# Linear attention on quarters of the array: keys by values, scores and state products without zero padding

## Chip, core and metric

The kernel runs on one core of one Trainium2 chip. The metric is the time of one execution on the device, in microseconds (us). The engines are named as the profile names them: PE is the tensor engine (PEld its weight loads), DVE the vector engine, ACT the scalar engine, POOL the general engine (GpSimd), SP the engine that issues most DMAs.

## What is computed

Two layers of a transformer over 256 latent tokens and 256 context tokens, width 1024. Each layer has a mixer of two parallel head groups (gated linear attention and neighbourhood attention), an output projection, and a channel mixer: dense in layer 0, the two best of eight experts in layer 1. The change touches the linear attention alone. Cut to that:

```python
def gla_chunk(q, k, v, g, s0):        # chunks of C = 64 tokens, 4 heads, dk = 64, dv = 128
    b = jnp.cumsum(g.reshape(B, H, n, C, dk), axis=3)
    b_ref = b[:, :, :, C // 2:C // 2 + 1, :]
    a = jnp.einsum('bhncd,bhnsd->bhncs', q * jnp.exp(b - b_ref), k * jnp.exp(b_ref - b))   # scores
    a = jnp.where(lower, a, 0.0)
    o = jnp.einsum('bhncs,bhnsv->bhncv', a, v)                                             # values
    b_last = b[:, :, :, -1:, :]
    ds = jnp.einsum('bhnsd,bhnsv->bhndv', k * jnp.exp(b_last - b), v)                      # keys by values
    # s <- exp(b_last) * s + ds over the chunks, from the context's last state on
    o = o + jnp.einsum('bhncd,nbhdv->bhncv', q * jnp.exp(b), s_prev)                       # state products
```

It is done in both directions (backward with the order flipped), the two outputs are added, and each head is normalised by its root mean square.

## The kernel before

The tokens stand in four blocks of 128 (`tt` 0 and 1 latent, 2 and 3 context), so a block holds two chunks, and the 128 partitions of a tile split at 64 into two chunks or two heads (`hpi` counts pairs of heads). `gla_parts` (L671) builds the linear attention; its generator `core` (L772) runs eight items, four steps by two directions `d`, with the blocks in the order 2, 3, 0, 1 forward and 3, 2, 1, 0 backward. An item has output where its block is in `qtts`: all eight in layer 0, the last four in layer 1, twelve together. For each item:

- `s0` splits the log gates into `ghi` and `glo`, `s1` sums them by matmul with constant triangles (L794, L804), turns the keys (L796), and makes `et`, `E` and `ke` on ACT and the products `klz`, `qez`, `ke` on DVE and `qb` on POOL. The names that end in z are padded: the two halves of the partitions are written into different columns, and the rest stays zero from a clearing at the start (`zt`, L680, with `zget` handing the cleared tiles out in turn).
- `s2` (L835) makes the scores into one bank of PSUM (L840), copies them under the causal mask into the cleared tile `aT` (L843), and makes keys by values into another bank (L849).
- `s3` (L866) takes a pair of items, one of each direction: `values` (L863) adds `aT` times `v` to the block's output bank, then for each of the two chunks the state products are added (L876) and `advance` (L886) makes the next state in a padded tile (L893 for the first, L895 afterwards). When both directions of a block are done, `normalise` (L900) empties its output bank.

The core is woven with the projections of the neighbourhood attention: `weave(G["core"](gc), chain(Stream(jobs).gen(), fill_core), 1)` (L1125) takes one step of projection work (L210 to L212, twelve passes of 512 columns) for each step of the core, and then, when those are used up, modulation work (L356). Apart from a few parts that are ordered by hand, the order within each engine's queue is made by a planner with a priority list, before the run and from its own costs; `s1` is marked urgent. PSUM has eight banks here, handed out from one pool (`ps`). Behind the core come the neighbourhood attention, the output projection and the channel mixer. The f32 operands of these matmuls are whole f32; L210 to L212 and the gate sums use a shorter form of f32 in split parts.

Of the kernel before, what the change touches and what calls it, by code (L numbers as in the profile page):

```python
# [9 lines left out]
F32 = mybir.dt.float32  # L10
# [6 lines left out]
P = 128  # L17
# [18 lines left out]
def make_consts():  # L36

    i = np.arange(P)
    s, c = i[:, None], i[None, :]
    same = (s // 64) == (c // 64)  # L40
    groups = {}

    def put(group, name, a):
        g = groups.setdefault(group, ([], {}))
        at = sum(x.shape[1] for x in g[0])
        a = np.asarray(a, np.float32)
        g[1][name] = (at, a.shape[1])
        g[0].append(a)

    put("base", "ident", np.eye(P))  # L50
    sel = np.zeros((P, 2))
    sel[i % 32 == 0, 0] = 1.0
    sel[i % 32 == 1, 1] = 1.0
    put("base", "sel", sel)
    put("base", "one", np.ones((P, 1)))
    put("base", "eps", np.full((P, 1), EPS))

    rot = np.zeros((P, P))
    for d in range(P):
# [12 lines left out]
    put("mix", "cos", cos)  # L72
    put("mix", "sin", sin)
    for nm, le, ref in (("F", s <= c, 32), ("B", s >= c, 31)):
        r = (c // 64) * 64 + ref
        le_ref = (s <= r) if nm == "F" else (s >= r)
        put("gla", "T" + nm, np.concatenate([(same & le) * 1.0 - (same & le_ref) * 1.0, (same & le) * 1.0], 1) / 16.0)
        put("gla", "R" + nm, (same & ~le) / 16.0)
    put("moe", "tri", s < c)
    put("moe", "iota", np.repeat(i[None, :], P, 0))  # L80
    put("moe", "fold", (s % 32) == np.arange(NE)[None, :])
    put("moe", "want", np.repeat(np.array([RANKS]), P, 0))
    return {k: (np.ascontiguousarray(np.concatenate(g[0], 1)), g[1]) for k, g in groups.items()}
# [10 lines left out]
def kernel(ctx: ExitStack, tc: tile.TileContext, A: dict, out: bass.AP):  # L94
# [576 lines left out]
    def gla_parts(l, full, qtts, nq_tok, C, W, mx, gl, nv, o_sb):  # L671
# [3 lines left out]
        v4 = gl.tile([P, 4, 512], F32, name="v4")  # L675
        v = [v4[:, tt, :] for tt in range(4)]

        zero = {}

        def zt(nm, shape, n):  # L680
            tiles = [gl.tile(shape, F32, name=f"{nm}_{i}") for i in range(n)]
            for t in tiles:
                nc.gpsimd.memset(t, 0.0)
            zero[nm] = [tiles, 0]

        def zget(nm):
            z = zero[nm]
            z[1] += 1
            return z[0][(z[1] - 1) % len(z[0])]

        zt("klz", [P, 2, 256], 2)
        zt("qez", [P, 2, 2, P], 2)
        zt("aT0", [P, 4, P], 1)
        zt("aT1", [P, 4, P], 1)
        zt("S0", [P, 2, 2, P], 2)
        zt("S1", [P, 2, 2, P], 2)

        def gates_load(ge):
            wlr = ge.tile([P, KD, 32], F32, name="wlr")
# [72 lines left out]
        def core(gc):  # L772
# [14 lines left out]
            def s1(it):  # L787
# [17 lines left out]
                                         start=i == 0, stop=i == 1)  # L805
                et = gc.tile([P, 256], F32, tag="et", bufs=2, name="et")
                nc.scalar.activation(et, pe[:, 0:256], AF.Exp)
                it["klz"] = klz = zget("klz")
                for c in range(2):
                    r = slice(64 * c, 64 * c + 64)  # L810
                    nc.vector.tensor_tensor(out=klz[r, c, :], in0=pe[r, 256:512], in1=et[r, :], op=ALU.mult)
                if not it["out"]:
                    E = gc.tile([P, 2, 2], F32, tag="Es", bufs=3, name="Es")
                    nc.scalar.activation(E, pb[:, 0:4].rearrange("p (a t) -> p a t", a=2), AF.Exp)
# [8 lines left out]
                at = P + (63 if d == 0 else 0)  # L823
                nc.vector.tensor_copy(Es, E[:, :, at:at + 65:64])
                it["dec"] = lambda hpi, c: Es[:, hpi, c:c + 1]
                it["qez"] = qez = zget("qez")
                for c in range(2):
                    r = slice(64 * c, 64 * c + 64)
                    nc.vector.tensor_tensor(out=qez[r, :, c, :], in0=qT[r, :, tok], in1=E[r, :, 0:P], op=ALU.mult)
                it["ke"] = En  # L830
                nc.vector.tensor_tensor(out=En, in0=kT[:, :, tok], in1=En, op=ALU.mult)
                it["qb"] = qb = gc.tile([P, 2, P], F32, tag="qb", bufs=3, name="qb")
                nc.gpsimd.tensor_tensor(out=qb, in0=qT[:, :, tok], in1=E[:, :, P:2 * P], op=ALU.mult)

            def s2(it):  # L835
                d, tt = it["d"], it["tt"]
                if it["out"]:
                    pa = ps()
                    for hpi in range(2):
                        nc.tensor.matmul(pa[:, hpi * 256:(hpi + 1) * 256], it["ke"][:, hpi, :],  # L840
                                         it["qez"][:, hpi].rearrange("p a t -> p (a t)"), start=True, stop=True)
                    it["aT"] = aT = zget(f"aT{d}")
                    nc.vector.copy_predicated(aT, W("T" + "FB"[d], P, P).bitcast(I32).unsqueeze(1).to_broadcast([P, 4, P]),  # L843
                                              pa.rearrange("p (a t) -> p a t", a=4))
                pd = ps()
                it["pdv"] = pdv = pd.rearrange("p (a c t) -> p a c t", a=2, c=2)
                for c in range(2):
                    for h in range(4):
                        nc.tensor.matmul(pdv[64 * (h % 2):64 * (h % 2) + 64, h // 2, c, :],  # L849
                                         it["klz"][:, c, h * 64:(h + 1) * 64], v[tt][:, h * P:(h + 1) * P],  # L850
                                         start=True, stop=True)

            def values(it):
                d, tt = it["d"], it["tt"]
                if it["out"]:
                    first = tt not in obank
                    if first:
                        obank[tt] = ps()
                        seen[tt] = 0
                    seen[tt] += 1  # L860
                    ob = obank[tt]
                    for h in range(4):
                        nc.tensor.matmul(ob[:, h * P:(h + 1) * P], it["aT"][:, h, :], v[tt][:, h * P:(h + 1) * P],  # L863
                                         start=first and h == 0, stop=False, skip_group_check=True)

            def s3(pair):  # L866

# [2 lines left out]
                for i in range(2):  # L870
                    cs = [(it, i if it["d"] == 0 else 1 - i) for it in pair]
                    for hpi in range(2):
                        for it, c in cs:
                            S = state[it["d"]]
                            if it["out"] and S is not None:
                                nc.tensor.matmul(obank[it["tt"]][64 * c:64 * c + 64, hpi * 256:(hpi + 1) * 256],  # L876
                                                 it["qb"][:, hpi, 64 * c:64 * c + 64], S[:, hpi].rearrange("p a t -> p (a t)"),
                                                 start=False, stop=False, skip_group_check=True)
                    for it, c in cs:
                        if it["step"] < 3 or i == 0:  # L880
                            advance(it, c)
                for it in pair:
                    if it["out"] and seen[it["tt"]] == 2 and it["tt"] in obank:
                        normalise(it["tt"], obank.pop(it["tt"]))

            def advance(it, c):  # L886
                d = it["d"]
                S, Sn = state[d], zget(f"S{d}")
                for hpi in range(2):
                    for h in range(2):  # L890
                        r = slice(64 * h, 64 * h + 64)
                        if S is None:
                            nc.vector.tensor_copy(Sn[r, hpi, h, :], it["pdv"][r, hpi, c, :])  # L893
                        else:
                            nc.vector.scalar_tensor_tensor(  # L895
                                out=Sn[r, hpi, h, :], in0=S[r, hpi, h, :], scalar=it["dec"](hpi, c)[r],
                                in1=it["pdv"][r, hpi, c, :], op0=ALU.mult, op1=ALU.add)
                state[d] = Sn

            def normalise(tt, bank):  # L900
                ob = bank.rearrange("p (h t) -> p h t", h=4)
                o4 = o_sb[tt].rearrange("p (h t) -> p h t", h=4)
                nc.scalar.activation(o4, ob, AF.Square)
                ss = gc.tile([P, 4], F32, tag="g_ss", bufs=1, name="g_ss")
                nc.vector.tensor_reduce(out=ss, in_=o4, axis=AX.X, op=ALU.add)
# [1235 lines left out]
```

## Time and profile before

| | before |
|---|---|
| time, median of 3 runs | 1880.4 us (1879.72 to 1882.68) |
| the profiled execution | 1879.96 us |
| its span (first to last instruction) | 1878.1 us |
| mean granted clock of PE | 0.984 of full speed |
| busy: PE, PEld, DVE, ACT, POOL | 1797.8, 1297.5, 1189.9, 922.7, 84.2 us |
| moved by DMA | 491.90 MB, mean 262 GB/s |

Busy time is the time in which an engine has at least one instruction under way. Matmuls are pipelined, so their durations overlap, and starts tell more than durations. The span is the profiled execution's own time without what lies before the first and behind the last instruction.

### The profile page before, as it was taken

The numbers are of one execution on the slowest core, as the hardware profiler recorded it, in microseconds if no ns is written. First come the engines' busy times: TensorE is split into PE (matmuls) and PEld (weight loads), VectorE is DVE, ScalarE is ACT, GpSimd is POOL, SyncE is SP. The second block draws the span as 40 slices with busy tenths as digits, with TensorE's granted clock in tenths as the row PEclk, the third lists the DMA queues.
The fourth block names the chain that finished last, engine by engine and source line by source line (L and its number), as shares of the span: only waits on it lengthen the run. The fifth ranks groups of instructions, "written<-read, shape, count | busy, mean of one in ns | idle before, by whom it ended". The sixth has DMA issues, their size and how long they took to land. (4 is left out here: it accounts for less than half of the span.)

```text
span 1878.1 us, 25461 instructions
## 1 busy us (share of the span) xinstructions
PE 1797.8 (96%) x8773; PEld 1297.5 (69%) x8773; DVE 1189.9 (63%) x1750; ACT 922.7 (49%) x1329; POOL 84.2 (4%) x103
## 2 busy tenths in 40 slices
PE   5999899999999998999899999999999999999995
PEld 3688566877788887787577853588886358888731
DVE  4457686478642345368879951599996249999701
ACT  3443376522222336443757831577774247777501
POOL 2100200110000002001000000000000000000000
PEclk8999999999999999999899999999999999999998
DMA  9432546267763332424299999999999999999996
GB/s 327 137 105 52 183 163 221 79 197 255 227 190 92 121 109 66 141 79 130 58 341 340 325 347 404 409 409 404 409 378 350 407 406 408 404 409 385 340 408 262
DMA packets 203321, 491.90 MB, mean 262 GB/s; under 512 B 29744, under 2 KB 71248, under 8 KB 203184
## 3 DMA queue, kind: packets, MB, share of 16 engines
q1 hardware_dynamic: 201152, 483.12, 71.0%
q0 software_dynamic: 2032, 7.08, 1.1%
q8 instruction: 71, 1.16, 0.3%
q14 instruction: 66, 0.54, 0.1%
HBM read 485.94 MB, written 4.98 MB: 261 GB/s over the span
## 5 line engine op out<-in xcount | busy, mean ns | idle before, releaser
L170 DVE TENSOR_TENSOR wl<-raw,wr 128x1024 fp32r<-128x1024 f32 x446 | 536.1, 1225 | 132.9 <-ACT wr L169 128.7
L169 ACT ACTIVATE wr<-raw 128x1024 fp32r<-128x1024 f32 x446 | 465.8, 1059 | 295.3 <-PE ps L211 152.0
L210 PE MATMUL ps<-wr,HR 128*128 128x512 f32 x736 | 299.3, 407 | 2.5 <-ACT wr L169 2.5
L211 PE MATMUL ps<-wl,HR 128*128 128x512 f32 x736 | 294.4, 400 | 7.5 <-DVE wl L170 6.5
L212 PE MATMUL ps<-wr,HL 128*128 128x512 f32 x736 | 292.3, 397 | 0.0
L210 PE MATMUL ps<-HR,wr 128*128 128x512 f32 (+1 forms) x592 | 220.3, 373 | 9.6 <-ACT HR L1979 6.2
L211 PE MATMUL ps<-HL,wr 128*128 128x512 f32 (+1 forms) x592 | 218.5, 369 | 3.4 <-POOL HL L521 1.7
L212 PE MATMUL ps<-HR,wl 128*128 128x512 f32 (+1 forms) x592 | 217.4, 367 | 0.5 <-DVE wl L170 0.5
L211 PEld LDWEIGHTS ps<-wl,HR 128*128 128x128 f32 x736 | 139.5, 190 | 47.0 <-DVE wl L170 14.7
L210 PEld LDWEIGHTS ps<-wr,HR 128*128 128x128 f32 x736 | 139.5, 190 | 40.5 <-issue 4.7
L212 PEld LDWEIGHTS ps<-wr,HL 128*128 128x128 f32 x736 | 139.2, 189 | 32.5
L210 PEld LDWEIGHTS ps<-HR,wr 128*128 128x128 f32 x592 | 111.6, 189 | 41.8 <-issue 8.6
L211 PEld LDWEIGHTS ps<-HL,wr 128*128 128x128 f32 x592 | 112.3, 190 | 23.6 <-DVE HL L1984 3.4
L212 PEld LDWEIGHTS ps<-HR,wl 128*128 128x128 f32 x592 | 112.4, 190 | 19.2 <-DVE wl L170 1.0
L1600 PE MATMUL ps<-raw,xw 128*64 128x512 f32 (+1 forms) x596 | 117.2, 536 | 2.2 <-DMA raw<-in_moe_w_gate 1.1
L1615 DVE TENSOR_TENSOR hid<-hid,ps 128x512 f32<-128x512 f32 (+1 forms) x47 | 31.3, 665 | 132.9 <-PE ps L1600 132.9
L210 PE MATMUL ps<-wr,tr 128*128 128x512 f32 x280 | 111.9, 400 | 0.0
L211 PE MATMUL ps<-wl,tr 128*128 128x512 f32 x280 | 110.6, 395 | 0.0
L212 PE MATMUL ps<-wr,tl 128*128 128x512 f32 x280 | 110.4, 394 | 0.0
L1600 PEld LDWEIGHTS ps<-raw,xw 128*64 128x64 f32 x596 | 40.7, 137 | 66.4 <-issue 53.3
L405 DVE SCALAR_TENSOR_TENSOR sums<-raw,condS,sums 128x512 f32<-128x512 f32 x98 | 71.6, 761 | 19.6 <-DMA raw<-in_w_ada 18.8
L1600 PE MATMUL ps<-raw,tw 128*64 128x512 f32 x272 | 67.2, 605 | 3.9 <-DMA raw<-in_moe_w_down 2.8
(368 smaller groups left out, 2433.6 us busy)
## 6 DMA issues: line engine op xcount, KB each, us to landing
raw<-in_moe_w_down SPq DMA_DIRECT2D x180, 512.0 KB
raw<-in_moe_w_gate SPq DMA_DIRECT2D x169, 512.0 KB
raw<-in_moe_w_up SPq DMA_DIRECT2D x167, 512.0 KB
raw<-in_w_ada SPq DMA_DIRECT2D x80, 512.0 KB
raw<-in_w_in SPq DMA_DIRECT2D x48, 512.0 KB
HR1w<-in_moe_w_up SPq DMA_DIRECT2D x24, 512.0 KB
raw<-in_ffn_w_gate SPq DMA_DIRECT2D x22, 512.0 KB
raw<-in_ffn_w_up SPq DMA_DIRECT2D x22, 512.0 KB
```

Source lines behind the costliest of these rows:

```text
L169: nc.scalar.activation(wr, raw, AF.Copy)
L170: nc.vector.tensor_tensor(out=wl, in0=raw, in1=wr.bitcast(F32), op=ALU.subtract)
L210: nc.tensor.matmul(o, lr, rr, start=start, stop=False)
L211: nc.tensor.matmul(o, lr, rl, start=False, stop=False)
L212: nc.tensor.matmul(o, ll, rr, start=False, stop=stop)
L405: nc.vector.scalar_tensor_tensor(out=o, in0=i_, scalar=s_, in1=o, op0=ALU.mult, op1=ALU.add)
L1600: nc.tensor.matmul(o[a * HALF:(a + 1) * HALF, 0:n], x, raw[:, a * n:(a + 1) * n], start=start, stop=stop)
L1615: nc.vector.tensor_tensor(out=hid, in0=hid, in1=st.pop((fb, 1))[:, 0:w], op=ALU.mult)
```

## The change

Score, key-value and state products are cut so that each matmul contracts over 64 partitions and writes 64 partitions: it uses a quarter of the array (a half of its rows by a half of its columns). What contracts over the lower half of the partitions goes to one PSUM bank and what contracts over the upper half to another. The padded tiles `klz`, `qez` and the padded states go; `aT` stays padded. Per item with output the scores are 8 matmuls of 64 columns instead of 2 of 256, key-value products 8 of 128 columns as before but over 64 partitions instead of 128, and the state products of one chunk and pair of heads 2 of 128 columns instead of 1 of 256. The scores share their two banks with the key-value products; the output of blocks `tt` and `tt + 1` shares two banks, split by head parity. A mask of 64 columns for each direction joins the constants.

```diff
+        put("gla", "M" + nm, le[:64, :64][i % 64] / 16.0)
...
-        zt("klz", [P, 2, 256], 2)
-        zt("qez", [P, 2, 2, P], 2)
-        zt("aT0", [P, 4, P], 1)
-        zt("aT1", [P, 4, P], 1)
-        zt("S0", [P, 2, 2, P], 2)
-        zt("S1", [P, 2, 2, P], 2)
+        keep = {}
+        for d in range(2):
+            keep[d] = gl.tile([P, 2, 2, P], F32, name=f"aT{d}")
+            nc.gpsimd.memset(keep[d], 0.0)
...
-                it["klz"] = klz = zget("klz")
-                for c in range(2):
-                    r = slice(64 * c, 64 * c + 64)
-                    nc.vector.tensor_tensor(out=klz[r, c, :], in0=pe[r, 256:512], in1=et[r, :], op=ALU.mult)
+                it["kl"] = et
+                nc.vector.tensor_tensor(out=et, in0=pe[:, 256:512], in1=et, op=ALU.mult)
...
-                it["qez"] = qez = zget("qez")
-                for c in range(2):
-                    r = slice(64 * c, 64 * c + 64)
-                    nc.vector.tensor_tensor(out=qez[r, :, c, :], in0=qT[r, :, tok], in1=E[r, :, 0:P], op=ALU.mult)
+                it["qe"] = qe = gc.tile([P, 2, P], F32, tag="qe", bufs=2, name="qe")
+                nc.vector.tensor_tensor(out=qe, in0=qT[:, :, tok], in1=E[:, :, 0:P], op=ALU.mult)
...
+            half = [slice(0, 64), slice(64, P)]
+
             def s2(it):
+
                 d, tt = it["d"], it["tt"]
+                banks = [ps() for _ in range(2)]
+                it["pdv"] = pdv = [b_[:, 0:256].rearrange("p (a t) -> p a t", a=2) for b_ in banks]
                 if it["out"]:
-                    pa = ps()
+                    pa = [b_[:, 256:384].rearrange("p (a t) -> p a t", a=2) for b_ in banks]
                     for hpi in range(2):
-                        nc.tensor.matmul(pa[:, hpi * 256:(hpi + 1) * 256], it["ke"][:, hpi, :],
-                                         it["qez"][:, hpi].rearrange("p a t -> p (a t)"), start=True, stop=True)
...
-                pd = ps()
-                it["pdv"] = pdv = pd.rearrange("p (a c t) -> p a c t", a=2, c=2)
-                for c in range(2):
-                    for h in range(4):
-                        nc.tensor.matmul(pdv[64 * (h % 2):64 * (h % 2) + 64, h // 2, c, :],
-                                         it["klz"][:, c, h * 64:(h + 1) * 64], v[tt][:, h * P:(h + 1) * P],
-                                         start=True, stop=True)
+                        for c in range(2):
+                            for a in range(2):
+                                nc.tensor.matmul(pa[a][half[c], hpi, :], it["ke"][half[a], hpi, half[c]],
+                                                 it["qe"][half[a], hpi, half[c]], start=True, stop=True)
+                    it["aT"] = aT = keep[d]
+                    mask = W("M" + "FB"[d]).bitcast(I32).unsqueeze(1).to_broadcast([P, 2, 64])
+                    for c in range(2):
+                        for a in range(2):
+                            nc.vector.copy_predicated(aT[half[c], :, a, half[c]], mask[half[c]], pa[a][half[c]])
+                for h in range(4):
+                    for c in range(2):
+                        nc.tensor.matmul(pdv[c][half[h % 2], h // 2, :], it["kl"][half[c], h * 64:(h + 1) * 64],
+                                         v[tt][half[c], h * P:(h + 1) * P], start=True, stop=True)
+
+            def o_bank(tt, a):
+
+                return obank[tt // 2][a][:, tt % 2 * 256:(tt % 2 + 1) * 256].rearrange("p (h t) -> p h t", h=2)
...
-                                nc.tensor.matmul(obank[it["tt"]][64 * c:64 * c + 64, hpi * 256:(hpi + 1) * 256],
-                                                 it["qb"][:, hpi, 64 * c:64 * c + 64], S[:, hpi].rearrange("p a t -> p (a t)"),
-                                                 start=False, stop=False, skip_group_check=True)
+                                for a in range(2):
+                                    nc.tensor.matmul(o_bank(it["tt"], a)[half[c], hpi, :], it["qb"][half[a], hpi, half[c]],
+                                                     S[half[a], hpi, :], start=False, stop=False, skip_group_check=True)
...
             def advance(it, c):
                 d = it["d"]
-                S, Sn = state[d], zget(f"S{d}")
-                for hpi in range(2):
-                    for h in range(2):
-                        r = slice(64 * h, 64 * h + 64)
-                        if S is None:
-                            nc.vector.tensor_copy(Sn[r, hpi, h, :], it["pdv"][r, hpi, c, :])
-                        else:
-                            nc.vector.scalar_tensor_tensor(
-                                out=Sn[r, hpi, h, :], in0=S[r, hpi, h, :], scalar=it["dec"](hpi, c)[r],
-                                in1=it["pdv"][r, hpi, c, :], op0=ALU.mult, op1=ALU.add)
+                S, Sn = state[d], gc.tile([P, 2, P], F32, tag=f"S{d}", bufs=2, name=f"S{d}")
+                if S is None:
+                    nc.vector.tensor_copy(Sn, it["pdv"][c])
+                else:
+                    for hpi in range(2):
+                        nc.vector.scalar_tensor_tensor(out=Sn[:, hpi, :], in0=S[:, hpi, :], scalar=it["dec"](hpi, c),
+                                                       in1=it["pdv"][c][:, hpi, :], op0=ALU.mult, op1=ALU.add)
...
-                nc.scalar.activation(o4, ob, AF.Square)
+                for a in range(2):
+                    nc.scalar.activation(o4[:, a], o_bank(tt, a), AF.Square)
...
-                nc.vector.tensor_tensor(out=o4, in0=ob, in1=y.unsqueeze(2).to_broadcast([P, 4, P]), op=ALU.mult)
+                for a in range(2):
+                    nc.vector.tensor_tensor(out=o4[:, a], in0=o_bank(tt, a),
+                                            in1=y[:, a:4:2].unsqueeze(2).to_broadcast([P, 2, P]), op=ALU.mult)
```

## Rows read from the trace of the kernel before

**Rows 1.** The page: the span, and the busy time of the tensor engine with its share of the span and its instructions.

```profile
span 1878.1 us, 25461 instructions
PE 1797.8 (96%) x8773; PEld 1297.5 (69%) x8773; DVE 1189.9 (63%) x1750; ACT 922.7 (49%) x1329; POOL 84.2 (4%) x103
```

**Rows 2.** Busy time by stretch: the two cores of the linear attention, and a stretch of the experts. The columns are the stretch, its length, the busy time of PE, PEld, DVE, ACT and POOL with their instructions, the granted clock, the busy share of the DMA engines, GB/s.

```profile
115.70:209.00 93.30, 93.30 (x585) 74.22 (x586) 62.95 (x145) 30.83 (x60) 8.60 (x12) 1.00 0.25 67
814.00:880.00 66.00, 66.00 (x488) 54.31 (x490) 48.34 (x110) 24.15 (x47) 4.00 (x6) 1.00 0.31 96
...
1200.00:1300.00 100.00, 100.00 (x444) 80.81 (x443) 91.46 (x85) 79.04 (x83) 0.00 (x0) 1.00 1.03 407
```

**Rows 3.** The instructions by tile, whole span: scores, key-value products and state products. The columns are the count of records, the duration in ns (least/median/most), first and last start, shapes.

```profile
L840 PE MATMUL ps<-qez,ke x48: 377/379/483, 131.5 to 874.3; 128*128 128x256 f32 x48
...
L849 PE MATMUL ps<-v,klz x256: 272/273/324, 132.5 to 875.4; 128*64 128x128 f32 x128
...
L876 PE MATMUL ps<-S,qb x88: 379/379/431, 147.3 to 879.4; 128*64 128x256 f32 x88
```

**Rows 4.** The tensor engine's instructions in order of time, layer 0. The columns are start, time from first start to last end, line, names, shapes and count of what is merged.

```profile
140.61 1.03 PE L840 MATMUL ps<-qez,ke 128*128 128x256 f32 x4
141.56 1.09 PE L849 MATMUL ps<-v,klz 128*64 128x128 f32 x16
142.59 0.50 PE L210 MATMUL ps<-HR,wr 128*128 128x512 f32 x1
142.93 0.40 PE L211 MATMUL ps<-HL,wr 128*128 128x512 f32 x1
...
145.46 1.95 PE L863 MATMUL ps<-v,aT 128*128 128x128 f32 x16
147.34 1.08 PE L876 MATMUL ps<-S,qb 128*64 128x256 f32 x8
148.35 0.50 PE L210 MATMUL ps<-HR,wr 128*128 128x512 f32 x1
...
171.62 1.95 PE L876 MATMUL ps<-S,qb 128*64 128x256 f32 x16
173.50 0.50 PE L210 MATMUL ps<-HR,wr 128*128 128x512 f32 x1
```

**Rows 5.** The same in a narrow window, 141.5 to 141.6 us.

```profile
141.56 0.33 PE L849 MATMUL ps<-v,klz 128*64 128x128 f32 x2
```

**Rows 6.** The same in layer 1, where key-value products of an item without output begin.

```profile
830.52 0.39 PE L211 MATMUL ps<-HL,wr 128*128 128x512 f32 x1
830.75 0.39 PE L212 MATMUL ps<-HR,wl 128*128 128x512 f32 x1
831.07 1.09 PE L849 MATMUL ps<-v,klz 128*64 128x128 f32 x16
```

**Rows 7.** The same in layer 1: gate sums with two columns and weights of 128 columns.

```profile
808.08 0.36 PE L804 MATMUL ps<-sums,ghi 128*128 128x2 f32 x2
808.30 0.36 PE L804 MATMUL ps<-sums,glo 128*128 128x2 f32 x2
```

**Rows 8.** The instructions of L807 (`et`), and what ended the scalar engine's idle time before them: us in total and times.

```profile
L807 ACT ACTIVATE et<-ps x16: 367/385/391, 116.8 to 866.2; 128x256 f32<-128x256 f32 x16
...
  PE ps L796: 34.5, 10
```

**Rows 9.** The vector engine's instructions on the tiles of the change, whole span; columns as in rows 3.

```profile
L811 DVE TENSOR_TENSOR klz<-ps,et x32: 409/422/428, 117.2 to 867.8; 64x256 f32<-64x256 f32 x32
...
L829 DVE TENSOR_TENSOR qez<-qT,E x24: 407/420/424, 119.0 to 868.7; 64x256 f32<-64x256 f32 x24
...
L843 DVE COPY_PREDICATED aT<-sums,ps x12: 732/741/747, 133.8 to 876.0; 128x512 f32<-128x512 int32 x12
...
L895 DVE SCALAR_TENSOR_TENSOR S<-S,Es,ps x96: 325/347/357, 138.7 to 877.7; 64x128 f32<-64x128 f32 x96
...
L893 DVE COPY S<-ps x16: 267/288/295, 137.4 to 834.3; 64x128 f32<-64x128 f32 x16
```

**Rows 10.** The tensor engine's instructions in order of time at the end of layer 0's core.

```profile
200.04 1.02 PE L840 MATMUL ps<-qez,ke 128*128 128x256 f32 x4
...
202.02 1.06 PE L356 MATMUL ps<-raw,condS 128*32 128x512 f32 x8
203.02 1.13 PE L840 MATMUL ps<-qez,ke 128*128 128x256 f32 x4
...
205.10 2.05 PE L863 MATMUL ps<-v,aT 128*128 128x128 f32 x16
207.09 1.95 PE L876 MATMUL ps<-S,qb 128*64 128x256 f32 x16
208.96 1.06 PE L356 MATMUL ps<-raw,condS 128*32 128x512 f32 x8
```

**Rows 11.** The squares of `normalise`; columns as in rows 3.

```profile
L903 ACT ACTIVATE x<-ps x6: 592/595/598, 173.6 to 880.3; 128x512 f32<-128x512 f32 x6
```

**Rows 12.** POOL in order of time, at the start of layer 1's mixer: the last cleared tiles but one, and a split of an activation.

```profile
733.15 1.45 POOL L683 MEMSET S<- 128x512 f32 x3
734.58 3.50 POOL L521 TENSOR_TENSOR HL<-n_h,HR 128x512 fp32r<-128x512 f32 x2
```

**Rows 13.** SP's DMA issues in order of time: the first loads of expert weights.

```profile
937.12 7.24 SPq L163 DMA_DIRECT2D raw<-in_moe_w_gate  x8
```

More of the change, by code (lines that the diff above doesn't have):

```diff
@@ L676, in gla_parts @@
         v = [v4[:, tt, :] for tt in range(4)]
[L678 to L689, printed above, removed]
-        zt("klz", [P, 2, 256], 2)
-        zt("qez", [P, 2, 2, P], 2)
-        zt("aT0", [P, 4, P], 1)
-        zt("aT1", [P, 4, P], 1)
-        zt("S0", [P, 2, 2, P], 2)
-        zt("S1", [P, 2, 2, P], 2)
+        keep = {}
+        for d in range(2):
+            keep[d] = gl.tile([P, 2, 2, P], F32, name=f"aT{d}")
+            nc.gpsimd.memset(keep[d], 0.0)
         def gates_load(ge):
@@ L839, in s2 @@
                     for hpi in range(2):
-                        nc.tensor.matmul(pa[:, hpi * 256:(hpi + 1) * 256], it["ke"][:, hpi, :],
-                                         it["qez"][:, hpi].rearrange("p a t -> p (a t)"), start=True, stop=True)
-                    it["aT"] = aT = zget(f"aT{d}")
-                    nc.vector.copy_predicated(aT, W("T" + "FB"[d], P, P).bitcast(I32).unsqueeze(1).to_broadcast([P, 4, P]),
-                                              pa.rearrange("p (a t) -> p a t", a=4))
@@ L855, in values @@
                 if it["out"]:
-                    first = tt not in obank
+                    first = tt // 2 not in obank
                     if first:
[L858 to L864, printed above, removed]
+                        obank[tt // 2] = [ps() for _ in range(2)]
+                    seen[tt] = seen.get(tt, 0) + 1
+                    for a in (1, 0):
+                        for hpi in range(2):
+                            h = 2 * hpi + a
+                            nc.tensor.matmul(o_bank(tt, a)[:, hpi, :], it["aT"][:, hpi, a, :], v[tt][:, h * P:(h + 1) * P],
+                                             start=first and hpi == 0, stop=False, skip_group_check=True)
             def s3(pair):
@@ L882, in s3 @@
                 for it in pair:
-                    if it["out"] and seen[it["tt"]] == 2 and it["tt"] in obank:
-                        normalise(it["tt"], obank.pop(it["tt"]))
+                    if it["out"] and seen[it["tt"]] == 2:
+                        seen[it["tt"]] = 3
+                        normalise(it["tt"])
             def advance(it, c):
                 d = it["d"]
-                S, Sn = state[d], zget(f"S{d}")
-                for hpi in range(2):
-                    for h in range(2):
-                        r = slice(64 * h, 64 * h + 64)
-                        if S is None:
-                            nc.vector.tensor_copy(Sn[r, hpi, h, :], it["pdv"][r, hpi, c, :])
-                        else:
-                            nc.vector.scalar_tensor_tensor(
-                                out=Sn[r, hpi, h, :], in0=S[r, hpi, h, :], scalar=it["dec"](hpi, c)[r],
-                                in1=it["pdv"][r, hpi, c, :], op0=ALU.mult, op1=ALU.add)
+                S, Sn = state[d], gc.tile([P, 2, P], F32, tag=f"S{d}", bufs=2, name=f"S{d}")
@@ L898, in advance, with normalise @@
+                if S is None:
+                    nc.vector.tensor_copy(Sn, it["pdv"][c])
+                else:
+                    for hpi in range(2):
+                        nc.vector.scalar_tensor_tensor(out=Sn[:, hpi, :], in0=S[:, hpi, :], scalar=it["dec"](hpi, c),
+                                                       in1=it["pdv"][c][:, hpi, :], op0=ALU.mult, op1=ALU.add)
                 state[d] = Sn
-            def normalise(tt, bank):
-                ob = bank.rearrange("p (h t) -> p h t", h=4)
-                o4 = o_sb[tt].rearrange("p (h t) -> p h t", h=4)
-                nc.scalar.activation(o4, ob, AF.Square)
+            def normalise(tt):
+                o4 = o_sb[tt].rearrange("p (h a t) -> p a h t", a=2, t=P)
+                for a in range(2):
+                    nc.scalar.activation(o4[:, a], o_bank(tt, a), AF.Square)
@@ L904, in normalise @@
                 ss = gc.tile([P, 4], F32, tag="g_ss", bufs=1, name="g_ss")
-                nc.vector.tensor_reduce(out=ss, in_=o4, axis=AX.X, op=ALU.add)
+                nc.vector.tensor_reduce(out=ss, in_=o_sb[tt].rearrange("p (h t) -> p h t", h=4), axis=AX.X, op=ALU.add)
                 y = rstd_of(gc, ss, 4, 1.0 / P)
-                nc.vector.tensor_tensor(out=o4, in0=ob, in1=y.unsqueeze(2).to_broadcast([P, 4, P]), op=ALU.mult)
+                for a in range(2):
+                    nc.vector.tensor_tensor(out=o4[:, a], in0=o_bank(tt, a),
+                                            in1=y[:, a:4:2].unsqueeze(2).to_broadcast([P, 2, P]), op=ALU.mult)
```

## The prediction

> **What bounds the kernel now.** I read the page first, then the busy time by stretch, then the tensor engine's instructions in order of time inside the two stretches that the change touches, then the vector engine's and the queues around them.
>
> The page gives a span of 1878.1 us with the tensor engine busy 96% of it [rows 1]. The profiled execution took 1879.96 us, 1.86 us more than its span and 0.44 us under the median of 1880.4 us; I work the sum against 1879.96 us. About 0.2% (3.8 us) is what a measurement of this kernel can tell from no change.
>
> The stretches tell where a gain would count [rows 2]. The linear-attention core runs from 115.7 to 209 us (layer 0) and from 814 to 880 us (layer 1). In both the tensor engine is busy without a gap (93.30 of 93.30 us, 66.00 of 66.00 us) at the full granted clock, 2.4 GHz, while the vector engine has 62.95 and 48.34 us of work and the DMA share is 0.25 and 0.31. So the tensor engine sets their length, and a microsecond of its work that goes is a microsecond of the stretch. From about 1000 us on the expert weights bound the kernel (DMA share 1.03 from 1200 to 1300 us), but their first loads are issued at 937.12 us [rows 13], behind both cores: what the cores save moves the whole expert part forward, and its length stays.
>
> **The unit of the sum.** Each f32 matmul stands in the trace as two passes: the scores of L840 are 24 matmuls in the program and 48 records, the key-value products of L849 128 and 256, the state products of L876 44 and 88 [rows 3]. Counts below are passes.
>
> What does a pass cost where halves of the array run side by side? Sixteen L863 passes on the whole array (128 columns) take 145.46 to 147.34, 0.1175 each. Eight L876 passes (256 columns, 64 weights wide) take 1.01 (147.34 to 148.35), sixteen take 1.88 (171.62 to 173.50): 0.87 for eight more, so a round of two passes is 0.2175 and 0.14 is fixed. Sixteen L849 passes (128 columns) take 1.03 (141.56 to 142.59); less 0.14 that is eight rounds of 0.11 [rows 4]. That two passes of a round run together is seen in a narrow window: two L849 passes fill 0.33 us, one of them up to 0.324 [rows 3, 5]. With four column groups of 32 it goes four wide: eight L356 passes of 512 columns take 1.00 (202.02 to 203.02) [rows 10], where eight on their own would take 8 x 4 x 0.1175 = 3.8. No row shows two row halves working side by side; that is the first unknown.
>
> Going into and out of the narrow forms costs too. An L849 group begins 0.32 behind the last whole-array pass (830.75 to 831.07) instead of 0.23 (830.52 to 830.75) [rows 6], so 0.09 at entry; 0.14 is inside, as above; and the first L210 afterwards lasts 0.34 instead of 0.23 (142.59 to 142.93) [rows 4], 0.11. A visit costs 0.34.
>
> **Scores, key-value products and their order (twelve items with output, eight in layer 0 and four in layer 1).** Before: 140.61 to 142.59 is 1.98, with the exit 2.09. After: 16 score passes of 64 columns in four rounds, 16 key-value passes of 128 columns in four rounds of 0.11. A score round lies between 0.055 and 0.11: streaming is half of 0.11, and the weights set a floor, since two-column passes with 128 columns of weights still start 0.11 apart (808.08 to 808.30, two of them) [rows 7], half of which I take for 64. I take 0.06, nearer the streaming row. Both parts now share two banks, and the masked copies must read the scores before the key-value products write the same bank: today `et` reads columns 0 to 255 of its bank, yet what ends its wait ten times is L796, which writes columns 256 to 511 of it [rows 8]. So the tensor engine leaves the narrow form between them and comes back, two visits: 2 x 0.34 + 4 x 0.06 + 4 x 0.11 = 1.36. Saved: 0.73, times 12, 8.8 us (8.8 + 0.2 to 8.8 - 2.4 for the bounds of the score round).
>
> The Trainium skill (TensorEngine Tiling (Array Packing), Instruction Overhead) speaks against the scores: some 60 cycles of overhead for each matmul, so that a dimension already small should not be split. By it sixteen passes would take, as an estimate at 2.4 GHz, 16 x 25 ns = 0.40 instead of 0.24, and the sum would be 1.9 us smaller. The trace does not agree for passes on different parts: the second L849 pass starts within 0.01 us of the first [rows 3, 5].
>
> **The four items without output (layer 1).** Eight rounds become four: 4 x 0.44 = 1.8 us.
>
> **State products.** 88 passes are 44 rounds of 0.2175; 176 passes of half the columns, four to a round, are 44 rounds of 0.11. Saved 44 x 0.1075 = 4.7 us. Values (L863) keep form and count.
>
> Gross: 8.8 + 1.8 + 4.7 = 15.3 us.
>
> **What is added, and its cover.** One masked copy of 0.74 becomes four on 64 partitions; the nearest rows, 64 x 128 with PSUM, take 0.29 (L893) and 0.35 (L895) [rows 9]. I take 0.35: 1.4 and a hand-over of 0.1 before the key-value products may start. In eight of the twelve items projection matmuls hide this: twelve passes of 0.23 make one step of 2.8 us. The copies can also queue behind a split of a weight on the vector engine, and the order was planned without knowing when they end. Below: nothing. Above: 8 x 2.7 = 21.6 us if nothing covers and a 1.2 us split stands ahead each time. The trace has the tensor engine fully covered now, so I take 0.25 an item, 2.0 us.
>
> The last pair of each core has no projection left. Today 200.04 to 208.96 is 8.92 us, all tensor work [rows 10]. Counted plainly it would become 8.92 - 2 x 0.73 - 8 x 0.1075 = 6.6. The chain scores (0.4), hand-over (0.1), eight copies (2.8), second key-value visit (0.7), values (1.99), states (1.0) gives 7.0; with slack I charge 0.5 for each core, 1.0 us.
>
> At each core's end two squares of 0.595 [rows 11] become four of half width, whose fixed part is paid twice more, and two tokens' outputs now share banks that both engines read. I charge 0.5 per core, 1.0 us (0 to 2).
>
> The vector engine loses work: half of the 32 `klz` and 24 `qez` products at 0.42, 48 of the 96 state updates at 0.35, three quarters of 16 copies [rows 9], against 36 more masked copies. None of it is priced, because no group of the tensor engine waits in these stretches. The cleared tiles that go are POOL's; in layer 1 POOL takes up its split 0.0 us behind the last of them (733.15 + 1.45, 734.58) [rows 12], so at most a few tenths are gained there. The constants grow by 128 columns, one copy of under 0.1 us.
>
> Net: 15.3 - 2.0 - 1.0 - 1.0 = 11.3; 1879.96 - 11.3 = **1868.7 us**.
>
> **Rivals.** *Row halves take turns* (0.18). Then scores need eight rounds (0.48), key-value eight (0.88), states 88 rounds of 0.11. An item is 0.68 + 0.48 + 0.88 = 2.04 against 2.09: nothing is won, the charges of 4.0 stay, about 1883.5 us (1879 to 1887). For it: no row shows row halves together. Against: column groups, four of them with four streams, do run together [rows 10].
>
> *The copies hold up the tensor engine* (0.08), which ends slower. Scores, copies and key-value products stand back to back in its queue; each item waits 1.5 us and whatever is ahead on the vector engine. One visit falls away (0.34 x 8 = 2.7), so it decides from (13.3 + 2.7) / 8 = 2.0 us an item; at 2.7 the time is 1879.96 + 21.6 - 16.0 = 1885.6 us. For it: the bank rule [rows 8]. Against: L849 groups are already broken up by other work. The Trainium skill (TensorEngine Tiling (Array Packing), PSUM Bottleneck) warns of this: tiling speeds the array but not what empties PSUM. No run here shows it yet.
>
> *All is covered* (0.10): no charges, score rounds at the floor, and the lighter vector engine shortens hand-overs: 1879.96 - 15.5 = 1864.5, down to 1858.
>
> *Given back later* (0.06): loads issued off the last filler work (202.02 and 208.96, L356 [rows 10]) set the next stage, so that the core's tail does not count: 1872 to 1879 us.
>
> **Numbers.** The forecast case has 0.58, alone 1862 to 1875. With the others the range is 1858 to 1884: it leaves out the ends of the first two rivals and little below. Faster by over 0.2%: 0.58 + 0.10 + half of the last, 0.70. Same 0.16, slower 0.14, mostly the first two rivals.
>
> **What would show it.** In the trace after: score and key-value passes starting in groups of four, 16 key-value passes in about 0.58; state groups of 32 in about 1.0; each core stretch shorter, layer 0 by about 7 us and layer 1 by about 4; first expert load near 926 us. Passes in pairs, a wait of the tensor engine on the masked copies, or a longer stretch from 209 to 235 us would make it wrong.

## The result, and the profile after

The changed kernel takes 1869.49 us (median of 4, 1868.96 to 1872.48) against 1881.07 us (1879.72 to 1882.68) for the kernel before on the same chip: a ratio of 0.9941, interval 0.9928 to 0.9954. The forecast was 1868.7 us. The profiled execution is the longest of the four, 1872.48 us. Lines are those of the changed kernel: scores L829, masked copies L835, key-value products L838, values L855, state products L869.

The page, to be read beside [rows 1]:

```profile
span 1870.7 us, 25857 instructions
PE 1784.4 (95%) x9005; PEld 1287.4 (69%) x9005; DVE 1161.8 (62%) x1704; ACT 922.9 (49%) x1335; POOL 75.4 (4%) x87
```

The two attention stretches by busy time (columns as in [rows 2]), from the first gate-sum pass to the last state pass:

```profile
118.20:205.10 86.90, 86.03 (x738) 67.42 (x740) 49.06 (x125) 31.14 (x62) 7.02 (x10) 1.00 0.29 72
803.60:870.90 67.30, 67.30 (x606) 55.70 (x607) 37.26 (x85) 26.97 (x52) 3.34 (x4) 1.00 0.34 101
```

Before, the same stretches ran from 115.77 to 209.03 us and from 806.79 to 879.77: 93.26 and 72.98 us. They are now 86.81 and 67.27 us (118.25 to 205.06, 803.61 to 870.88), 6.4 and 5.7 us less. The vector engine's 62.95 us [rows 2] is down to 49.06. Two later traces of the changed kernel (experiments 1 and 6 below) show the same two lengths within 0.1 us.

An item of layer 0 in order of time on the tensor engine (start, time to the last end, line, names), beside [rows 4]:

```profile
186.61 0.39 PE L213 MATMUL ps<-HR,wl 128*128 128x512 f32 x1
186.93 0.46 PE L829 MATMUL ps<-qe,ke 64*64 64x64 f32 x16
187.32 0.51 PE L211 MATMUL ps<-HR,wr 128*128 128x512 f32 x1
187.66 0.40 PE L212 MATMUL ps<-HL,wr 128*128 128x512 f32 x1
...
188.36 0.39 PE L212 MATMUL ps<-HL,wr 128*128 128x512 f32 x1
188.68 0.67 PE L838 MATMUL ps<-v,et 64*64 64x128 f32 x16
189.28 0.50 PE L213 MATMUL ps<-HR,wl 128*128 128x512 f32 x1
...
193.81 1.10 PE L869 MATMUL ps<-S,qb 64*64 64x128 f32 x32
194.84 0.50 PE L211 MATMUL ps<-HR,wr 128*128 128x512 f32 x1
```

From a group's start to the next instruction: scores 0.39 us, key-value products 0.60 (1.03 before), state products 1.03 (1.88 before). Four passes now share a round. Projection passes stand between scores and products, so an item enters the narrow form twice. The waits of the tensor engine in layer 0's stretch (who waited for whom, us in total, times, the longest); layer 1's has none:

```profile
PE ps L838 <- DVE aT L835: 0.9, 2, 0.6
```

Outside these stretches the change moves two more things. GpSimd clears eight tiles fewer, so its two transfers of 1.5 MB that fill a bias table (L334; L333 before, issued at 6.4 us) go out at 2.92 us, among the first loads. POOL in order of time:

```profile
1.96 0.43 POOL L332 MEMSET far<- 128x384 f32 x1
2.44 0.52 POOL L940 MEMSET ql<- 64x512 f32 x1
2.92 2.03 POOL L334 DMA_DIRECT2D rel<-far  x2
```

The low-rank passes that end the first stretch start at 67.25 us instead of 64.78. And after the first expert load, at 926.61 us instead of 937.12 [rows 13], part of the lead of 10.5 us goes: the first expert matmul comes 168.4 us later, before 165.7. Twenty microseconds from that stretch, first before, then after (columns as in [rows 2]):

```profile
957.10:977.10 20.00, 15.85 (x88) 12.60 (x87) 15.24 (x39) 10.31 (x22) 1.37 (x2) 0.83 0.81 280
```

```profile
946.60:966.60 20.00, 16.17 (x83) 12.68 (x84) 14.31 (x42) 8.96 (x21) 1.37 (x2) 0.70 0.75 252
```

The mean granted clock is 0.70 instead of 0.83 of 2.4 GHz. As an estimate, (0.83 - 0.70) x 20 = 2.6 us at full clock are missing there; that these are the 2.7 us is not shown (see the part on the prediction).

### The profile page after: what moved, and what is told of

Read it like the earlier page. It is cut to its first block, busy times and chain, and to the rows that moved or that the text cites. A ratio compares the mean times of both kernels' runs of the same rounds, so it can differ in the third digit from the quotient of the medians.

```text
span 1870.7 us, 25857 instructions
## 1 busy us (share of the span) xinstructions
PE 1784.4 (95%) x9005; PEld 1287.4 (69%) x9005; DVE 1161.8 (62%) x1704; ACT 922.9 (49%) x1335; POOL 75.4 (4%) x87
## 5 line engine op out<-in xcount | busy, mean ns | idle before, releaser
L171 DVE TENSOR_TENSOR wl<-raw,wr 128x1024 fp32r<-128x1024 f32 x446 | 535.1, 1222 | 140.6 <-ACT wr L170 137.1
```

What stands on the lines that cost most here:

```text
L171: nc.vector.tensor_tensor(out=wl, in0=raw, in1=wr.bitcast(F32), op=ALU.subtract)
```

## The experiments

All times are medians, with ratios to the kernel before measured on the same chip. The changed kernel itself, the neighbour of experiments 1 to 3, took 1868.67 us (ratio 0.9936, 0.9923 to 0.9949); the neighbour of 6 and 7, 1868.41 us (0.9950, 0.9936 to 0.9964). "Stretch" is as above; in these two runs it is 86.9 us in layer 0 and 67.2 to 67.3 in layer 1.

**1. The row halves in turns.** The loop over row halves goes outermost:

```
-for hpi in range(2):
-    for c in range(2):
-        for a in range(2):          # scores, row half a
+for a in range(2):
+    for hpi in range(2):
+        for c in range(2):
...
-for h in range(4):
-    for c in range(2):              # products, row half c
+for c in range(2):
+    for h in range(4):
```

and the state products likewise.

> The changed kernel with the same quarter matmuls, but ordered so that one half of the rows has all its passes before the other half. Theory (rounds of four quarters are the gain): rounds double. 12 items x 4 score rounds x 0.058 = 2.8, 16 x 4 key-value rounds x 0.11 = 7.0, 44 state rounds x 0.11 = 4.8, together 14.6 us: 1884 us (1880 to 1887), 16 key-value passes taking about 1.03 instead of 0.60. Rival (the gain came from the lighter vector engine and the missing padding): within 2 us of the changed kernel.

1875.17 us (0.9972, 0.9962 to 0.9982), 6.5 us slower: neither figure. The stretches take 91.6 and 69.7 us. The tensor engine in order of time:

```profile
188.18 0.47 PE L829 MATMUL ps<-qe,ke 64*64 64x64 f32 x16
...
190.36 0.66 PE L838 MATMUL ps<-v,et 64*64 64x128 f32 x8
190.94 0.50 PE L211 MATMUL ps<-HR,wr 128*128 128x512 f32 x1
...
195.93 1.16 PE L869 MATMUL ps<-S,qb 64*64 64x128 f32 x32
197.02 0.50 PE L211 MATMUL ps<-HR,wr 128*128 128x512 f32 x1
```

The edit undid the concurrency only in part. Eight products of one row half take 0.58 us (190.36 to 190.94), nearly as long as sixteen in the changed kernel: that is the price of two to a round. But scores (0.40) and state products (1.09) hardly lost, although written in turns: passes of the other row half ran beside them. So the run shows what the products lose when their halves part. Whether the other passes overtook one another or the planner had already put them in another order than the written one is open: the records do not name the quarter of a pass.

**2. The vector engine's work put back.** The products with `et` and `qe` and the state updates by row halves again, as the padded kernel had them; the masked copies stay four to an item, so the vector engine now has 66.3 us of work in layer 0's stretch, 3.3 more than in the kernel before:

```
-nc.vector.tensor_tensor(out=qe, in0=qT[:, :, tok], in1=E[:, :, 0:P], op=ALU.mult)
+for r in half:
+    nc.vector.tensor_tensor(out=qe[r], in0=qT[r, :, tok], in1=E[r, :, 0:P], op=ALU.mult)
```

> The changed kernel's matmuls, with the vector engine's work of the kernel before put back: key and query products in two halves of the partitions, each state update in four pieces of 64 partitions instead of two of 128, first states likewise. That is some 25 us of vector work more. Theory (the tensor engine sets the stretch): 0 to 1.5 us over the changed kernel. Rival (the lighter vector engine gave the gain): 5 to 11 us over it.

1879.1 us (0.9991, 0.9980 to 1.0002): 10.4 us slower, the rival's time, and the gain is gone. The stretches take 89.5 and 74.2 us, together 9.6 more than in the changed kernel. The waits for the copies are 2.6 us in layer 0 and 4.0 in layer 1 (0.9 and none in the changed kernel). The tensor engine in layer 1 (here scores are L831, products L840, copies L837, state updates L889), and the vector engine over the same time:

```profile
856.02 0.46 PE L831 MATMUL ps<-qe,ke 64*64 64x64 f32 x16
...
857.46 0.28 PE L213 MATMUL ps<-HR,wl 128*128 128x256 f32 x1
861.38 1.33 PE L840 MATMUL ps<-v,et 64*64 64x128 f32 x16 [3.64 <-DVE aT L837]
862.65 0.58 PE L211 MATMUL ps<-HR,wr 128*128 128x256 f32 x1
```

```profile
855.24 1.23 DVE L171 TENSOR_TENSOR wl<-raw,wr 128x1024 fp32r<-128x1024 f32 x1 [2.77 <-ACT wr L170]
...
857.42 0.85 DVE L798 TENSOR_TENSOR et<-ps,et 64x256 f32<-64x256 f32 x2
858.20 0.41 DVE L815 TENSOR_TENSOR qe<-qT,E 64x256 f32<-64x256 f32 x1
858.62 0.43 DVE L817 TENSOR_TENSOR ke<-kT,ke 128x256 f32<-128x256 f32 x1
859.07 1.42 DVE L889 SCALAR_TENSOR_TENSOR S<-S,Es,ps 64x128 f32<-64x128 f32 x4
860.52 1.01 DVE L837 COPY_PREDICATED aT<-sums,ps 64x128 f32<-64x128 int32 x4
```

The scores are done by 856.5 us, but their four copies stand behind the split of a projection weight (L171) and the eight pieces shown after it, and begin at 860.52; the products, which write the copies' bank, wait 3.64 us. The split was itself late, since the vector engine stood idle for 2.77 us until its weight was there. So the queue ahead of the copies, and not the pieces alone, makes this wait; a split ahead of the copies is what the prediction's upper bound named. After the idle time of the tensor engine sixteen products take 1.27 us instead of 0.60. The granted clock of the next 6.7 us is 0.58, most of it at the lower level of 1.2 GHz (columns as in [rows 2]):

```profile
861.30:868.00 6.70, 6.62 (x47) 6.17 (x51) 4.32 (x11) 1.97 (x5) 0.00 (x0) 0.58 0.27 78
868.00:874.00 6.00, 5.68 (x104) 4.24 (x101) 5.74 (x17) 1.33 (x2) 0.74 (x1) 1.00 0.15 22
```

The lower clock costs some (1 - 0.58) x 6.7 = 2.8 us there, as an estimate from that row. With the 5.7 us of waits more than in the changed kernel this makes 8.5 of the 9.6 us. So the lighter vector engine is what keeps the hand-over of the shared bank hidden. The Trainium skill (TensorEngine Tiling (Array Packing), PSUM Bottleneck) says that tiling speeds the tensor engine but not what empties PSUM; this run agrees, at 3.64 us in one place.

**3. Products ahead of the scores.** In `s2` the key-value products are issued first; nothing they write is then read by a copy before them.

> The changed kernel with the key-value products put ahead of the scores in each item, so that they need not wait for the masked copies and one visit to the quarter form is enough for both. Theory (a visit costs 0.34 us and the waits on the copies 0.9 in all): 12 x 0.34 + 0.9 = 5.0 us less, 1864.5 us (1862 to 1867). Rival (the visits are hidden, or what the core saves here is given back behind it): 1868 to 1871 us.

1864.96 us (0.9921, 0.9909 to 0.9933), 3.7 us less: inside the expected range, though the interval overlaps the changed kernel's. A second time, as the neighbour of experiments 4 and 5: 1866.11 us (0.9927, 0.9912 to 0.9941). In it layer 0's stretch is 82.9 us, 4.0 less than in the changed kernel, and an item is one visit to the narrow form (products L826, scores L833), 0.83 us to the next instruction instead of 0.39 + 0.60 and a second entry and exit:

```profile
182.28 0.67 PE L826 MATMUL ps<-v,et 64*64 64x128 f32 x16
182.77 0.41 PE L833 MATMUL ps<-qe,ke 64*64 64x64 f32 x16
183.11 0.50 PE L211 MATMUL ps<-HR,wr 128*128 128x512 f32 x1
```

Layer 1's stretch, where the theory had put four of its twelve visits, gains nothing (67.9 us): its last values wait 1.4 us for the copies, which are now issued later.

**4. Products first, and the vector work back.** The edits of 2 and 3 together.

> Keys-by-values passes ahead of the scores, and the vector engine's work put back as it was before the change: the query, key and state updates by row halves, some 13 us more of its work in layer 0 and 12 us in layer 1. Theory (the lighter vector engine matters only because the keys-by-values passes wait for the masked copies of the scores in their bank; with the order turned round nothing of the tensor engine waits for the copies except the values' tail): 0 to 3 us over the same order with the light vector work, 1865 to 1868, and the stall of about 3.6 us before the products in layer 1 is gone. Rival (the vector engine sets the length of the stretch by itself, through gates, decays and states): about 10 us over it, 1875, as it was when the same work was put back with the scores first, and the waits stand before other passes: scores, state passes or values.

1867.65 us (0.9938, 0.9926 to 0.9951), 1.5 us over its neighbour, the theory's time, and not to be told from it. In layer 0 the theory holds throughout, 83.9 us and no wait for the copies. In layer 1 it holds by half: the long stall before the products is gone, but its stretch is 5.0 us longer (72.9), with other waits, as the rival said:

```profile
PE ps L857 <- DVE aT L841: 4.0, 3, 1.7
PE ps L828 <- DVE S L889: 1.3, 1, 1.3
PE ps L782 <- DVE S L889: 0.7, 1, 0.7
```

Part of these 5 us is regained behind the stretch (2.6 us remain in the span).

**5 (two kernels). The transfers of the bias table.** Built on 3: the two score tiles are cleared five times over, which puts the transfers back to 6.7 us; and `clear_rel` is written after the low-rank step.

```
-        clear_rel(sp)
...
     G["low_rank"](ge)
+    if full:
+        clear_rel(ge)
```

> Keys-by-values passes ahead of the scores, and GpSimd sets the two score tiles to zero five times over instead of once: eight more sets of 128 x 512, as many as the kernel before spent on tiles that the change drops. They stand ahead of the two transfers of 1.5 MB that set the bias table in memory to its floor, so these go out near 6.4 us again and not at 2.9. Theory (the change let these two transfers go out ahead of the first loads of x and of the conditioning weights): the second group of x passes starts near 11.2 us again and not near 12.1, the low-rank passes of layer 0 start near 64.8 us and not near 66.3, and the time is 1 to 2 us less than the neighbour with one set, 1863 to 1864. Rival (the late start comes from something else, the loads of the first stretch sharing the rate of memory whatever the order): low-rank passes at 66 and the same time as the neighbour within 0.7 us.

> Keys-by-values passes ahead of the scores, and the two transfers that set the bias table to its floor are written after the low-rank step, behind the first stretch of loads. They move 3.15 MB, 12.7% of the sixteen engines' time in the first 60 us, at a time in which the transfers run at some 350 to 410 GB/s. Theory (the first stretch is bound by the loads): the low-rank passes of layer 0 start 4 to 8 us earlier, near 58 to 62 us, and the time falls by 3 to 8 us against the neighbour, to 1857 to 1862. Rival (the tensor engine and the scalar engine set the first stretch, or the transfers only move into the stretch of the bias table and the next loads): less than 1.5 us.

With the extra clears: 1867.66 us (0.9925, 0.9913 to 0.9938), not to be told from its neighbour, though the low-rank passes start at 63.75 us instead of 65.78 and the wait for the conditioning weights `w_ada` ahead of them falls from 6.6 us to 3.7. The first half of the theory holds; the 2 us do not reach the end (3.0 us ahead at the first expert matmul, 0.3 in the span; in one slice of the experts the granted clock is 0.95 against 0.97). Written behind the loads, the transfers are issued at 50.39 and 53.89 us, that wait is gone, and the low-rank passes start 8.8 us earlier:

```profile
50.39 1.13 POOL L334 DMA_DIRECT2D rel<-far  x1 [0.31 <-POOL far L332]
...
53.89 0.92 POOL L334 DMA_DIRECT2D rel<-far  x1
```

```profile
56.98 0.62 PE L701 MATMUL ps<-HR,wlr 128*32 128x512 f32 x1
```

1859.58 us (0.9886, 0.9872 to 0.9900), 6.5 us less. So the loads bind the first stretch: 3.15 MB fewer ahead of them, and the wait for them goes.

**6. Scores on the whole array again.** The rest as changed; padded queries, one masked copy for an item, a bank of their own.

> The changed kernel with its scores as they were before: four passes of 256 columns over the whole array into a bank of their own, queries padded by row half, one masked copy for an item instead of four; keys by values and state products stay on quarters. Theory (the scores on quarters are worth their passes: an item's scores took 0.95 us ahead of the products and now take 0.39 us and an entry of some 0.09; 12 items; against that the waits for the masked copies go, some 1.5 us): 2.5 to 5 us slower than the changed kernel, 1871 to 1873.5, of it some 3 us in layer 0. Rival (what the scores' passes gain is paid again by the bank that they share with the products and by the second entry, so that quarters for the scores are worth nothing): within 1 us of the changed kernel, or faster.

1867.0 us (0.9934, 0.9920 to 0.9947): not to be told from the changed kernel. Its stretches are 87.1 and 69.3 us, 0.1 and 2.0 longer; in layer 1 the tensor engine waits 1.4 us for a state update, which it does not in the changed kernel. By line in layer 0 (busy us, mean ns), first here, then the changed kernel:

```profile
L832 PE MATMUL ps<-qez,ke 128*128 128x256 f32 x32 | 8.3, 382 | 0.0
L840 PE MATMUL ps<-v,et 64*64 64x128 f32 x128 | 6.2, 283 | 0.0
```

```profile
L838 PE MATMUL ps<-v,et 64*64 64x128 f32 x128 | 5.9, 282 | 0.9 <-DVE aT L835 0.9
L829 PE MATMUL ps<-qe,ke 64*64 64x64 f32 x128 | 4.7, 231 | 0.0
```

The scores' passes are 3.6 us shorter on quarters, and layer 0 is 0.1 us shorter. By the prices above, eight second visits (8 x 0.34 = 2.7) and the waits (0.9) take the rest. In time the rival holds; in layer 1 the changed kernel's stretch is the shorter one, and that does not show at the end.

**7. Scores in two banks of their own.** The order as changed.

```
-pa = [b_[:, 256:384].rearrange("p (a t) -> p a t", a=2) for b_ in banks]
+pa = [ps()[:, 0:128].rearrange("p (a t) -> p a t", a=2) for _ in range(2)]
```

> The changed kernel with the scores' two halves in two banks of their own, so that the products, still written after the scores, have no masked copy to wait for; four banks for an item instead of two. Theory (the copies in the shared bank hold the products up, and the scores' second entry is a cost of its own that stays): the waits of 0.9 us in layer 0 and the long products of 0.80 us there are gone, 1 to 2 us faster than the changed kernel, 1867 to 1868, and not as fast as the kernel with the products first. Rival (the pool of banks runs short: the scores or the values wait for a bank to come free): new waits of the tensor engine in the two stretches, 0 to 5 us slower than the changed kernel.

1861.37 us (0.9910, 0.9895 to 0.9925), 7.0 us less, far more than expected. No group of the change waits for a copy any more. The rival's shortage of banks shows only as 0.9 us: one projection pass of layer 0 waits 0.6 us for a copy to empty a bank, one score group of layer 1 waits 0.3 us for the scalar engine to do so. Stretches 83.3 and 65.7 us, 5.3 us less together; the rest of the gain lies behind them, where the way from the end of layer 1's stretch to the first expert matmul is 1.7 us shorter. Here scores and products of an item stand together, so my theory's premise, that the second entry stays, was wrong:

```profile
183.95 0.46 PE L829 MATMUL ps<-qe,ke 64*64 64x64 f32 x16
184.23 0.62 PE L838 MATMUL ps<-v,et 64*64 64x128 f32 x16
184.78 0.51 PE L211 MATMUL ps<-HR,wr 128*128 128x512 f32 x1
```

The shared bank is what parted them.

**8. Own banks and the late transfers.** The edits of 7 and of the second kernel of 5.

> The two separate gains together: the scores in two banks of their own (order as in the changed kernel), and the two transfers of the bias table's floor written behind the low-rank step. Theory (the one is the tensor engine's in the two attention stretches, the other the first loads', so they add): 7 us for the banks and 6.5 us for the transfers below the changed kernel's 1868.5, 1855 us (1852 to 1858), with the first stretch ending near 57 us and layer 0's stretch in some 83.3 us. Rival (the earlier start meets the loads or the clock later, and part is given back): 1858 to 1861.

1856.15 us (0.9873, 0.9855 to 0.9890). The gains add to within about 1 us; of the kernels run this one is the fastest, some 12 us below the changed one (which was not run on this chip).

## Why the prediction was right, and where its steps were not

**The unit prices held.** Two row halves do work side by side, the first unknown. Predicted from two-wide rows: score group 0.38, key-value group 0.58, state group of 32 passes 1.02; measured 0.39, 0.60, 1.03. The entry is 186.61 to 186.93, 0.32, and the first whole-array pass afterwards 0.34, as in [rows 4, 6]. An item costs 0.39 + 0.60 + 2 x (0.09 + 0.11) = 1.39 where 1.36 was predicted, and the gross is 12 x 0.70 + 4 x 0.43 + 4.7 = 14.8 us for 15.3. Of sixteen score passes, 0.39 less the fixed 0.14 leaves 0.25, where 0.24 was taken. The estimate of 0.40 that the prediction worked out from the Trainium skill (TensorEngine Tiling (Array Packing), Instruction Overhead) adds the 60 cycles of every pass one after another; the trace does not agree, at 0.25.

**The charges held in sum.** The stretches lost 6.4 + 5.7 = 12.1 us, so 14.8 - 12.1 = 2.7 went into hand-overs and tails, for 3.0 taken; only 0.9 of it is seen as a wait, the rest is not traced further. A masked copy lasts 0.30, not 0.35. The layers share the gain more evenly than the 7 and 4 named. Layer 0's last pair, from its first scores to the last state pass, takes 7.2 us (197.80 to 204.99) for the 6.6 + 0.5 taken. The charge of 1.0 for the squares is not seen: two of half width take 0.66 us together (205.15 us) where one took 0.595 [rows 11], and from layer 0's last state pass to the first scores of the neighbourhood attention it is 7.3 us where it was 7.7.

**The close hit is partly luck.** The forecast fall was 11.3 us, the medians fell by 11.6. What lies outside the stretches was priced at 1.0 us, for the squares, and it moves by more than the agreement. In the three traces of the changed kernel layer 0 begins 1.0 to 2.5 us later than before, the way from layer 0's stretch to layer 1's takes 594.8 to 598.6 us (597.8 in the one trace before), the way to the first expert load is 1.6 to 1.7 us shorter and the way from there to the first expert matmul 2.7 us longer. The spans fell by 7.4, 11.1 and 12.7 us, with 12.1 or 12.2 us in the stretches each time.

**The step that failed is the vector engine's.** "None of it is priced, because no group of the tensor engine waits in these stretches" judged the new kernel by the waits of the old. In the old one the products had a bank of their own. The change makes them wait for the masked copies, and with the vector work in its old pieces this wait, with the lower clock behind it, eats the whole gain (experiment 2). The rival "the copies hold up the tensor engine" was a real mechanism at 0.08, and what kept it small was the term priced at nothing. Neither was compared with the other. A wait on the masked copies was also named as a sign that would make the forecast wrong. It came, 0.9 us in two places, while the sum itself charged 2.0 for it: the sign was set too strictly.

**The shared bank was priced but not weighed.** Two visits for an item (0.34 x 12 = 4.1 us) and 2.0 for the hand-over stood in the sum. Experiment 7 takes both away and shortens the stretches by 5.3 us, near those 6.1. What the sum did not ask is whether the quarters for the scores are worth that: no gain from them can be told in the time (experiment 6), unless the bank changes too (experiment 7), or in layer 0 the order (experiment 3).

**The cleared tiles were looked at in the wrong place.** I followed POOL into layer 1 and expected a few tenths. What lay behind the clearings in its queue at the start were two transfers of 1.5 MB, and the low-rank passes start 1.0 to 2.5 us later in the changed kernel's traces. Experiment 5 shows the place; how much of it reaches the end is not settled.

**The lead did not move whole through the experts' loads.** 2.7 us of it went between the first expert load and the first expert matmul. The twenty microseconds shown above have a granted clock of 0.83 in the kernel before and in experiments 1, 2 and 4, whose lead is cut by 0.1 to 0.8 us there. They have 0.66 to 0.76 in the changed kernel and all others, whose lead is cut by 1.7 to 2.7 us. The lower clock and the lost lead go together, but not in size: experiment 7 has 0.66 and loses 1.7 us, the changed kernel 0.69 or 0.70 and loses 2.7. What sets either was not tried.

## To carry to other kernels

When a change packs two results into one bank, ask which engine must read the one before the other may be written, and what stands ahead of that read; a bank apart was worth 7.0 us here, while no gain from packing the scores could be told without it. A helper engine without waiters in the old profile is not free in the new one if the change adds a hand-over to it. Setup work that goes lets whatever is behind it in its queue start earlier, transfers too.

## What the hardware showed that was not expected

- Four passes on four quarters start together: in the changed kernel four score passes from 186.93 us fill 0.29 us together, where one of them lasts 0.27 at most. Passes written in turns by row half still overlap (experiment 1: state groups 1.09 us against 1.03).
- One idle time of 3.64 us was followed by passes at the lower of the two clock levels (products 1.27 us instead of 0.60), so this stall cost more than its length: layer 1's stretch grew by 7.0 us with 4.0 us of waits.
